# Split halves for a gated linear attention's gates, and the order of two feed-forward heads

## The chip, the cores and the metric

The kernel runs on one core of one Trainium2 chip. Its time is the device time of one execution in microseconds (us). The core has five engines, which the profile calls PE (TensorE, matrix products; its weight loads are listed as PEld), DVE (VectorE), ACT (ScalarE), POOL (GpSimd) and SP (SyncE, which here only issues DMA transfers). Each has its own queue of instructions and takes them in order; they wait for one another through semaphores.

## The reference

The reference is a trunk of four layers over 512 rows of 1024 numbers. A layer adds a mixer and then a feed-forward network (FFN) to `x`, each on a normalised copy. The mixers are S5 (layers 0 and 3), gated linear attention (GLA, layer 1) and differential attention (layer 2). All is in float32. What the change touches:

```python
def swiglu_ffn(h, w_gate_up, w_down):
    g, u = jnp.split(h @ w_gate_up, 2, axis=-1)
    return (jax.nn.silu(g) * u) @ w_down

# in gla_mixer: chunks of 64 rows, 4 heads with 128 keys and 256 values each
log_a = jax.nn.log_sigmoid((a_lo @ w_a2 + b_a).astype(f32)) / GLA_TEMP
cum = jnp.cumsum(log_a.reshape(shp_k), axis=2)
tot = cum[:, :, -1]
k_dec = k * jnp.exp(tot[:, :, None] - cum)
upd = jnp.einsum('bnchk,bnchv->bnhkv', k_dec, v)
decay = jnp.exp(tot)
# state = decay * state + upd, chunk after chunk; o = q @ state
```

`a_lo` has 16 columns; `w_a2` is 16 x 512 and `b_a` has 512 numbers. The FFN's hidden width is 2816.

## The kernel before

**Split halves.** A float32 operand is split into a high half (a cast to the type float32r, on ScalarE, line 420) and a low half (the rest, a subtraction on VectorE, line 428). A product is then three matmuls: high by high, high by low, low by high (`mm3`, lines 448 to 450; `seven_product`, line 594). Halves of weights lie in `whl`, which has five buffers. Weights come as raw tiles by DMA, some of them summed in the transfer (an accumulating DMA from POOL, lines 626 and 759).

**Seven products for eight.** The FFN's first matrix product and GLA's projection run in blocks of 256 columns by a scheme of Strassen's kind: seven quarter products, which the code calls one to seven, in place of eight. Each takes 24 matmuls of 256 columns. The left side's quarters and their sums (sides 11, 12, 22, and the totals 1 to 4) are made once; each block splits its own weights 11, 1, 21, 22 and 3, adds 22 to weight 1 and splits it again (S in the plans), adds 21 and splits it a third time (F). A suffix a, b or c names block 0, 1 or 2, and `one:a` is block a's product one, `one_out:a` its way out of the accumulator. In an FFN a block ends in `scale1` and `silu1` (first gate half), `gate2` (scale and silu of the second), `three_out` and `times` (gate by value, for each half) and `parts`, which splits the result into `act` for the down projection (`gemm_b`).

**The order of the work.** A planner orders every engine's instructions at compile time from a model of their costs, by the order in which the code emits them. Between `hand(...)` calls the engines that it names follow the emitted order exactly. `issue_after` ties an instruction behind another one on its engine. Each FFN begins with a plan written out by hand, the string `plan` in `ffn` (blocks a and b, engines PE, ACT, DVE, SP and POOL), and then a second one, which brings in block c and the gates of a and b (PE, ACT and DVE); from block c's `six` on the planner decides. FFNs 0 and 3 are called `glued`: they lay out their memory in another way.

**GLA.** Blocks 0 and 1 of the projection follow a plan of their own; from there on the order of TensorE alone is written out, and `block(b, out, between)` runs seven products with steps of the attention between them. Block 2 makes half the keys (`kd`), block 3 the values of two heads (`v1`). The gate steps: `alo` is `a_lo` turned, 32 rows because both halves of its weights are stacked; `decays` multiplies it by `w_a2` (line 2284, a plain float32 matmul over 128 rows, most of them zero or one) and takes Abs, Exp and Ln for the log-sigmoid; `sums` finishes that into `la`. `totals` forms each chunk's total with 16 matmuls that have `la` standing still and a two-column indicator `ind` streaming (line 2308), which gives them with the keys in partitions, as `dec` needs them; `later` forms the suffix sums with a triangular `mask` standing still and `la` streaming (line 2299) and multiplies the keys by their exponentials. `updates` and `readout` are the recurrence.

**FFN 2** also turns `x` and `r` through DRAM (`turn_x`, POOL), since S5 behind it wants its rows in another order. The side sum `total("3")` of that FFN is made at the end of the attention (line 2798).

Of the kernel before, what the change touches and what calls it, by code (L numbers as in the profile page):

```python
# [22 lines left out]
P = 128  # L23
D = 1024
# [316 lines left out]
class Trunk:  # L341
# [387 lines left out]
    def seven_block(self, fp, slots, left, wgu, b, turn, na):  # L729
# [35 lines left out]
        third = lambda name: self.np_.tile([P, 512], F32, tag="h", name=name) if b == 2 else T(name)  # L765
# [120 lines left out]
    def ffn(self, l, left, after=None, turn=False, aside=None, small=None):  # L886
# [7 lines left out]
        with self.tc.tile_pool(name=f"ffn{l}", bufs=1, reuse_waits="tile") as fp:  # L894
# [12 lines left out]
            blocks = [self.seven_block(fp, slots, left, wgu, b, turn, na) for b in range(FFN_HIDDEN // 256)]  # L907
# [10 lines left out]
            if l == 2:  # L918
                plan = """
                    split21a one:a split21b square flush one:b total1 one_out:a finish high1 low1 total2 split1a  # L920
# [3 lines left out]
                    high22 low22 three:a add21a highFa add21b lowFa highFb three:b lowFb seven_out:b scale1:a four:a  # L924
                    four:b
                """
            else:
# [6 lines left out]
                """  # L934
            def turned():
                nonlocal r
                r = self.turn_x(left.r) if turn else r
# [21 lines left out]
            self.planned(plan, left, f, more)  # L959
# [3 lines left out]
            for nb in (4, 4, 3) if na == 4 else (3, 3, 3, 2):  # L963
                acts = []
                for n in range(b0, b0 + nb):
                    b = blocks[n]
                    if n > 2:
                        loads(b)
                        for step in ("one", "one_out", "five", "five_out"):
                            b[step]()  # L970
                        b["add"]("22")
# [6 lines left out]
                    with self.tc.issue_after(behind["low"].ins) if n < 2 else nullcontext():  # L978
                        acts.append(b["parts"]())
# [1125 lines left out]
    def gla(self, l, left, after):  # L2105
# [5 lines left out]
        with self.tc.tile_pool(name="gla", bufs=1, reuse_waits="tile") as p:  # L2111
# [8 lines left out]
            on = [None, room("N", "on1")]  # L2120
# [33 lines left out]
            class Rows:  # L2154
# [17 lines left out]
                def stt(_, th, half, ps, f, op):  # L2172
                    for t, o, y in _.each(th, half, ps):
                        v.scalar_tensor_tensor(o, y, f[:, t : t + 1], o, op0=ALU.mult, op1=op)
# [32 lines left out]
            nc.gpsimd.dma_start(xd[:, :, 512:], self.x[:, :, 512:])  # L2207
# [36 lines left out]
            aT, wa2 = flat[:, :512], flat[:, 512:1024]  # L2244
# [7 lines left out]
            for n in (32, 64, 96):  # L2252
                v.memset(aT[n : n + 32], 1.0)
            nc.gpsimd.memset(wa2, 0.0)
            nc.sync.dma_start(wa2[0:16], i["gla_w_a2"][0])
            nc.sync.dma_start(wa2[16:32], i["gla_w_a2"][0])
            nc.sync.dma_start(wa2[32:33], i["gla_b_a"][0:1])
# [11 lines left out]
            v.tensor_tensor(aT[:32], ap_[:32], R[:32], op=ALU.mult)  # L2269
# [3 lines left out]
            on[0] = room("B", "on0")  # L2273
            la = room("D", "la")
# [3 lines left out]
            logs = []  # L2278

            def decays():  # L2280
                zs = [row(bank) for bank in four("z")]
                es = [flat[:, 1024 + t * 512 : 1536 + t * 512] for t in range(NT)]
                for t, (z, e) in enumerate(zip(zs, es)):
                    nc.tensor.matmul(z, aT[:, t * P : (t + 1) * P], wa2[:], start=True, stop=True)
# [7 lines left out]
            def sums():  # L2292
                with self.tc.issue_after(self.last["rows"].ins):
                    for t, (z, e) in enumerate(logs):
                        v.scalar_tensor_tensor(la[:, t], z, 0.0, e, op0=ALU.min, op1=ALU.subtract)

            def later():
                for t, bank in enumerate(four("suf")):
                    nc.tensor.matmul(row(bank), mask[:], la[:, t], start=True, stop=True)
# [4 lines left out]
            def totals():  # L2304
                dps = self.tp("dps")
                for t in range(NT):
                    for h in range(4):
                        nc.tensor.matmul(
                            dps[:, t, 2 * h : 2 * h + 2], la[:, t, h * P : (h + 1) * P], ind[:], start=True, stop=True
                        )  # L2310
                src = dps[:, :, :8].rearrange("p t (h c) -> p t h c", c=2)
                nc.scalar.activation(dec[:], src, AF.Exp, scale=1.0 / 16.0)
# [99 lines left out]
            block(2, Rows(kd, None, True), (decays, pause, sums, pause, pause, totals))  # L2412
            vs[1] = room("D", "v1")
            block(3, Rows(vs[1]), (later, pause, *core(0)))
# [83 lines left out]
    def diff(self, l, left, after):  # L2498
# [4 lines left out]
        with self.tc.tile_pool(name="diff", bufs=1) as p:  # L2503
# [289 lines left out]
            for t in range(2):  # L2793
# [4 lines left out]
                3: {1: (one,), 3: (one, lambda: nxt[0].total("3")), 5: (one,)},  # L2798
# [68 lines left out]
```

## Time and profile before

| | us |
|---|---|
| median of 3 runs (2232.98 to 2233.42) | 2233.0 |
| the profiled execution | 2241.29 |
| its span, first to last instruction | 2239.5 |
| TensorE busy | 2177.8 |
| VectorE busy | 1629.1 |
| ScalarE busy | 1139.5 |

The mean granted TensorE clock was 0.996 of full speed. Stages by TensorE's rows: S5 to about 207 us, FFN 0 to 567, GLA to 778, FFN 1 to 1120, differential attention to 1394, FFN 2 to 1737, S5 to 1895, FFN 3 to 2231.

How to read the rows: a timeline row has a start (us from the span's start), a length, the engine, the code line, the operation, what it writes and reads, the shape and a count; rows that follow one another are merged. The bracket at its end is the engine's idle time before it and who ended that. TensorE's matmuls overlap one another, so what one costs is read from start to start. A row of a chain gives start, length and what ran or was waited for.

### The profile page before, as it was taken

Reading aid. Unit: us, or ns where it says so; the run is one execution under the profiler, and the core shown is the slowest. Engines: PE = TensorE matmul, PEld = TensorE weight load, DVE = VectorE, ACT = ScalarE, POOL = GpSimd, SP = SyncE. Lnnn points to the kernel's source line nnn. Section 1 sums busy time; section 2 is a strip of 40 time slices with the busy share of each in tenths; the row PEclk is TensorE's granted clock in tenths of the full one; section 3 lists DMA queues with packets and bytes.
Section 4 is the critical chain, followed back from the end, with each engine's and each line's share of the span. In section 5 each row is a group of like instructions: output and inputs, shape, how many; then the busy total and the mean of one; then the engine's idle time right before and its main releaser. Section 6 shows DMA issues by size and latency. Waiting matters only on the chain.

```text
span 2239.5 us, 38455 instructions
## 1 busy us (share of the span) xinstructions
PE 2177.8 (97%) x15433; PEld 1973.2 (88%) x15433; DVE 1629.1 (73%) x2497; ACT 1139.5 (51%) x1835; POOL 330.0 (15%) x441
## 2 busy tenths in 40 slices
PE   6999999999999999999999999899999999999998
PEld 5888889989988898999888888899998888989997
DVE  9965978777978598876745676877766965967675
ACT  8644635445555455564435675644544334535343
POOL 3401142340111010100002221100000001101000
PEclk9999999999999999999999999999999999999999
DMA  4357667665763675765337455975631546856532
GB/s 92 63 172 179 180 156 195 161 172 169 175 141 113 155 183 171 178 186 129 94 129 166 108 134 150 248 194 132 179 95 57 155 147 160 199 159 166 164 76 76
DMA packets 309181, 333.63 MB, mean 149 GB/s; under 512 B 70477, under 2 KB 253033, under 8 KB 308874
## 3 DMA queue, kind: packets, MB, share of 16 engines
q1 hardware_dynamic: 238970, 238.93, 34.7%
q0 software_dynamic: 70032, 92.23, 21.9%
q8 instruction: 122, 2.00, 0.4%
q14 instruction: 57, 0.47, 0.1%
HBM read 297.16 MB, written 18.75 MB: 141 GB/s over the span
## 4 chain that ended last, share of the span: by engine, by line
PE 78%; DVE 10%; ACT 4%; issue 3%; DMA 3%; SPq 1%; POOL 0%; DVEq 0%; ACTq 0%; POOLq 0%
PE a L594 20%; PE acc L448 10%; PE acc L450 10%; PE acc L449 10%; PE c L594 10%; PE d L594 5%; DVE whl L428 3%; PE y L1651 2%; PE acc L1687 2%; ACT whl L420 2%; DMA halves<-in_ffn_w_gate_up_dram 1%; PE op L2650 1%; PE s L2617 1%; PE tp L117 1%; PE V L1607 1%
## 5 line engine op out<-in xcount | busy, mean ns | idle before, releaser
L428 DVE TENSOR_TENSOR whl<-wst,whl 128x1024 fp32r<-128x1024 f32 x260 | 316.6, 1223 | 213.4 <-ACT whl L420 209.9
L594 PE MATMUL a<-side,whl 128*128 128x256 f32 x3240 | 396.2, 279 | 10.2 <-DVE whl L428 7.4
L420 ACT CAST whl<-wst 128x1024 fp32r<-128x1024 f32 x260 | 272.2, 1051 | 241.7 <-PE acc L450 153.5
L594 PEld LDWEIGHTS a<-side,whl 128*128 128x128 f32 x3240 | 382.1, 189 | 13.9 <-DVE whl L428 9.5
L448 PE MATMUL acc<-whl,act 128*128 128x512 f32 x704 | 276.2, 392 | 0.4 <-DVE g L770 0.2
L449 PE MATMUL acc<-whl,act 128*128 128x512 f32 x704 | 274.6, 390 | 0.0
L450 PE MATMUL acc<-whl,act 128*128 128x512 f32 x704 | 274.4, 390 | 0.0
L594 PE MATMUL c<-side,whl 128*128 128x256 f32 x2160 | 261.3, 277 | 4.4 <-ACT whl L420 4.4
L594 PEld LDWEIGHTS c<-side,whl 128*128 128x128 f32 x2160 | 253.0, 188 | 5.0 <-ACT whl L420 5.0
L428 DVE TENSOR_TENSOR whl<-slot,whl 128x1024 fp32r<-128x1024 f32 x105 | 127.7, 1221 | 61.6 <-ACT whl L420 61.0
L448 PEld LDWEIGHTS acc<-whl,act 128*128 128x128 f32 x704 | 132.1, 188 | 29.3 <-DVE x L576 0.9
L450 PEld LDWEIGHTS acc<-whl,act 128*128 128x128 f32 x704 | 132.2, 188 | 27.6
L449 PEld LDWEIGHTS acc<-whl,act 128*128 128x128 f32 x704 | 132.2, 188 | 26.4
L420 ACT CAST whl<-slot 128x1024 fp32r<-128x1024 f32 x105 | 109.9, 1052 | 84.9 <-PE acc L450 44.6
L594 PE MATMUL a<-sides,whl 128*128 128x256 f32 x1080 | 132.9, 278 | 1.0 <-DVE x L576 1.0
L428 DVE TENSOR_TENSOR whl<-halves,whl 128x1024 fp32r<-128x1024 f32 x87 | 105.8, 1222 | 37.4 <-ACT whl L420 37.1
L420 ACT CAST whl<-halves 128x1024 fp32r<-128x1024 f32 x87 | 90.8, 1050 | 81.2 <-DVE halves L824 35.7
L594 PE MATMUL d<-sides,whl 128*128 128x256 f32 x1080 | 131.1, 278 | 0.0
L594 PEld LDWEIGHTS a<-sides,whl 128*128 128x128 f32 x1080 | 128.3, 188 | 2.2 <-issue 1.4
L594 PEld LDWEIGHTS d<-sides,whl 128*128 128x128 f32 x1080 | 127.5, 188 | 0.0
L759 POOL DMA_DIRECT2D wst<-in_ffn_w_gate_up_dram x44 | 57.1, 1297 | 463.8 <-DMA wst<-in_ffn_w_gate_up_dram 206.9
L877 ACT CAST act<-r 128x512 fp32r<-128x512 f32 (+1 forms) x110 | 66.7, 644 | 97.6 <-DVE r L853 80.5
(511 smaller groups left out, 4030.5 us busy)
## 6 DMA issues: line engine op xcount, KB each, us to landing
wst<-in_ffn_w_gate_up_dram SPq DMA_DIRECT2D x88, 512.0 KB, 4.9
wst<-in_ffn_w_down_dram SPq DMA_DIRECT2D x88, 512.0 KB, 4.5
slot<-in_ffn_w_gate_up_dram SPq DMA_DIRECT2D x69, 512.0 KB, 6.3
wst<-in_ffn_w_gate_up_dram POOLq DMA_DIRECT2D x44, 512.0 KB, 6.0
halves<-in_ffn_w_gate_up_dram SPq DMA_DIRECT2D x42, 512.0 KB, 6.1
wst<-in_s_w_glu_dram SPq DMA_DIRECT2D x32, 512.0 KB, 4.7
wst<-in_diff_w_qkv_dram SPq DMA_DIRECT2D x24, 512.0 KB, 4.9
slot<-in_ffn_w_gate_up_dram POOLq DMA_DIRECT2D x18, 512.0 KB, 8.9
```

The costliest lines, as they stand in the source:

```text
L117: tr.nc.tensor.transpose(p[:, j], h[:, j * P : (j + 1) * P], tr.ident[:])
L420: self.last["high"] = self.nc.scalar.copy(hl[:, 0], w[:])
L428: self.last["low"] = self.nc.vector.tensor_tensor(hl[:, 1], w[:], hl[:, 0].bitcast(F32), op=ALU.subtract)
L448: mm(out, lh, rh, start=first, stop=False)
L449: mm(out, lh, rl, start=False, stop=False)
L450: self.last["mm"] = mm(out, ll, rh, start=False, stop=last)
L594: mm(o, *two, start=first and not (j or k or n), stop=k == 3 and n == 2, skip_group_check=True,)
L759: nc.gpsimd.dma_start(w[:], left.quarter(*plus, b), accum_op=ALU.add)
L877: self.last["act high"] = nc.scalar.copy(dst[:, 0, j], src[:, j])
L1607: mm(V[kk][z][:, bs(b)], inm[:, z, bs(b)], U[:, bs(b)], start=True, stop=True)
L1651: mm(yb[:, b], q[:, j, b], om[:, j // 2, bs(b)], start=False, stop=j == 3)
L1687: mm(accs[t][:], zT[:, m // 2, kk, t * P : (t + 1) * P], hl[:, m % 2, kk % 2], start=kk == 0 and m == 0, stop=kk == KT - 1 and m == 2,)
```

## The change

In FFNs 1 and 2 the second written plan is dropped. In FFN 1 the first plan's end is reordered: scale and silu of both blocks come before the sum and splits for `four`, `three_out` of both after `four`; behind it come `gate2`, `times` and `parts` of a, then of b, then all of block c, in the planner's hands. In FFN 2 scale, silu and `three_out` are drawn into the first plan in the same way, behind the splits; then block c's loads and the split of its weight 1 come before gate a, its products one and five, the sum and the second split before gate b. Block c's results use the FFN's own buffers there. `total("3")` moves from the attention's end into FFN 2's plan. FFNs 0 and 3 keep both plans.

In GLA the gates, totals and suffix sums become products on split halves. `aT` stacks the high half, the low half and the high half of `a_lo`, and two rows of ones; `wa2` stacks high, high and low halves of the weights and both halves of the bias, so that one matmul over 98 rows per row tile gives the gates. The log gates are split into `lhi` and `llo` (`highs` on ScalarE, `lows` on VectorE, between blocks 2 and 3). The totals are formed with an eight-column window of the indicator standing still and 512 columns of `lhi` and `llo` streaming, eight matmuls that add up to an 8 x 512 tile, chunks in rows; its exponential is turned by four small transposes (`spread`). They move from block 2, behind its product three, to block 3, behind its product one, ahead of the suffix sums, which take two matmuls per tile in place of one.

```diff
@@ -726,7 +726,7 @@
-    def seven_block(self, fp, slots, left, wgu, b, turn, na):
+    def seven_block(self, fp, slots, left, wgu, b, turn, na, glued):
@@ -762,7 +762,7 @@
-        third = lambda name: self.np_.tile([P, 512], F32, tag="h", name=name) if b == 2 else T(name)
+        third = lambda name: self.np_.tile([P, 512], F32, tag="h", name=name) if glued and b == 2 else T(name)
@@ -904,7 +904,7 @@
-            blocks = [self.seven_block(fp, slots, left, wgu, b, turn, na) for b in range(FFN_HIDDEN // 256)]
+            blocks = [self.seven_block(fp, slots, left, wgu, b, turn, na, glued) for b in range(FFN_HIDDEN // 256)]
@@ -917,12 +917,12 @@
-                    split21a one:a split21b square flush one:b total1 one_out:a finish high1 low1 total2 split1a
+                    split21a one:a split21b square flush one:b total3 total1 one_out:a finish high1 low1 total2 split1a
...
-                    high22 low22 three:a add21a highFa add21b lowFa highFb three:b lowFb seven_out:b scale1:a four:a
-                    four:b
+                    high22 low22 three:a add21a highFa add21b lowFa highFb three:b lowFb seven_out:b scale1:a silu1:a four:a
+                    scale1:b silu1:b four:b three_out:a three_out:b
@@ -932,6 +932,13 @@
                 """
+            if l == 1:
+                a = plan.index("seven_out:b")
+                plan = plan[:a] + """
+                    seven_out:b scale1:a silu1:a scale1:b silu1:b add21a high22 low22 three:b highFa add21b lowFa highFb
+                    lowFb four:a four:b three_out:a three_out:b
+                """
+
             def turned():
@@ -956,7 +963,8 @@
-            self.planned(plan, left, f, more)
+            if glued:
+                self.planned(plan, left, f, more)
@@ -964,7 +972,18 @@
                     b = blocks[n]
-                    if n > 2:
+                    if not glued and n < 2:
+                        if l == 2 and n == 0:
+                            loads()
+                            blocks[2]["split"]("1")
+                        if l == 2 and n == 1:
+                            for step in ("one", "one_out", "five", "five_out"):
+                                blocks[2][step]()
+                            blocks[2]["add"]("22")
+                            blocks[2]["split"]("1")
+                        for step in ("gate2", "times"):
+                            b[step]()
+                    if n > 2 or l == 1 and n == 2:
                         loads(b)
@@ -975,7 +994,7 @@
                             b[step]()
-                    with self.tc.issue_after(behind["low"].ins) if n < 2 else nullcontext():
+                    with self.tc.issue_after(behind["low"].ins) if glued and n < 2 else nullcontext():
                         acts.append(b["parts"]())
@@ -2117,7 +2136,7 @@
-            on = [None, room("N", "on1")]
+            on = [None, None]
@@ -2171,7 +2190,9 @@
-                        v.scalar_tensor_tensor(o, y, f[:, t : t + 1], o, op0=ALU.mult, op1=op)
+                        self.last["added"] = v.scalar_tensor_tensor(
+                            o, y, f[:, t : t + 1], o, op0=ALU.mult, op1=op
+                        )
@@ -2204,7 +2225,7 @@
-            nc.gpsimd.dma_start(xd[:, :, 512:], self.x[:, :, 512:])
+            begun = nc.gpsimd.dma_start(xd[:, :, 512:], self.x[:, :, 512:])
@@ -2241,7 +2262,6 @@
-            aT, wa2 = flat[:, :512], flat[:, 512:1024]
@@ -2249,12 +2269,26 @@
-            for n in (32, 64, 96):
-                v.memset(aT[n : n + 32], 1.0)
-            nc.gpsimd.memset(wa2, 0.0)
-            nc.sync.dma_start(wa2[0:16], i["gla_w_a2"][0])
-            nc.sync.dma_start(wa2[16:32], i["gla_w_a2"][0])
-            nc.sync.dma_start(wa2[32:33], i["gla_b_a"][0:1])
+            exact = lambda y: y.bitcast(F32R)
+            zpart = whole(room("N", "zpart"))
+            aT, wa2, win, inner = (zpart[:, a:b] for a, b in ((0, 512), (512, 1024), (1024, 1038), (1040, 1168)))
+            wraw, araw = flat[:, 3072:3584], flat[:, 3584:4096]
+            wlow = self.sp.tile([P, 2], F32, tag="ms2", name="wlow", bufs=4)
+            nc.gpsimd.memset(araw[96:128], 1.0)
+            with self.tc.issue_after(begun.ins):
+                nc.gpsimd.memset(wlow[64:96, 0:1], -1.0)
+                nc.gpsimd.tensor_scalar_mul(wlow[96:128, 0:1], self.ident[96:128, 97:98], -1.0)
+            wa = i["gla_w_a2"][0]
+            nc.sync.dma_start(
+                wraw[0:96], bass.AP(tensor=wa.tensor, offset=wa.offset, ap=[[0, 6], [512, 16], [1, 512]])
+            )
+            nc.sync.dma_start(wraw[96:98], i["gla_b_a"][0].partition_broadcast(2))
+            nc.scalar.copy(exact(wa2[:98]), wraw[:98])
+            v.scalar_tensor_tensor(
+                wraw[64:98], wa2[64:98], wlow[64:98, 0:1], wraw[64:98], op0=ALU.mult, op1=ALU.add
+            )
+            nc.scalar.copy(exact(wa2[64:98]), wraw[64:98])
+            nc.scalar.copy(exact(aT[96:98]), araw[96:98])
@@ -2266,22 +2300,25 @@
-            v.tensor_tensor(aT[:32], ap_[:32], R[:32], op=ALU.mult)
+            v.tensor_tensor(araw[:32], ap_[:32], R[:32], op=ALU.mult)
+            for n in (0, 64):
+                nc.scalar.copy(exact(aT[n : n + 32]), araw[:32])
+            v.tensor_tensor(exact(aT[32:64]), araw[:32], aT[:32], op=ALU.subtract)
...
-            on[0] = room("B", "on0")
-            la = room("D", "la")
+            lhi, llo = room("D", "lhi"), room("B", "llo")
...
+            tot = flat[:8, 512:1024]
...
-                    nc.tensor.matmul(z, aT[:, t * P : (t + 1) * P], wa2[:], start=True, stop=True)
+                    nc.tensor.matmul(z, exact(aT[:98, t * P : (t + 1) * P]), exact(wa2[:98]), start=True, stop=True)
@@ -2292,24 +2329,44 @@
-                        v.scalar_tensor_tensor(la[:, t], z, 0.0, e, op0=ALU.min, op1=ALU.subtract)
+                        v.scalar_tensor_tensor(e, z, 0.0, e, op0=ALU.min, op1=ALU.subtract)
+                    v.tensor_copy(exact(inner), mask[:])
+                    v.tensor_scalar_mul(exact(win), mask[:, :14], 0.0)
+                    v.tensor_copy(exact(win[:, 6:8]), ind[:])
+
+            def highs():
+                for t in range(NT):
+                    nc.scalar.copy(exact(lhi[:, t]), logs[t][1])
+
+            def lows():
+                for t in range(NT):
+                    v.tensor_tensor(exact(llo[:, t]), logs[t][1], lhi[:, t], op=ALU.subtract)
...
+                totals()
...
-                    nc.tensor.matmul(row(bank), mask[:], la[:, t], start=True, stop=True)
+                    for z, y in enumerate((lhi, llo)):
+                        nc.tensor.matmul(row(bank), exact(inner), exact(y[:, t]), start=z == 0, stop=z == 1)
...
-                dps = self.tp("dps")
+                dps = row(self.tp("dps"))[:8]
...
-                    for h in range(4):
+                    for z, y in enumerate((lhi, llo)):
...
-                            dps[:, t, 2 * h : 2 * h + 2], la[:, t, h * P : (h + 1) * P], ind[:], start=True, stop=True
+                            dps, exact(win[:, 6 - 2 * t : 14 - 2 * t]), exact(y[:, t]),
+                            start=not (t or z), stop=t == NT - 1 and z == 1,
...
-                src = dps[:, :, :8].rearrange("p t (h c) -> p t h c", c=2)
-                nc.scalar.activation(dec[:], src, AF.Exp, scale=1.0 / 16.0)
+                nc.scalar.activation(tot, dps, AF.Exp, scale=1.0 / 16.0)
+
+            def spread():
+                dps = self.tp("dct")
+                for h in range(4):
+                    nc.tensor.transpose(dps[:, h, :8], tot[:, h * P : (h + 1) * P], self.ident[:8, :8])
+                v.tensor_copy(dec[:], dps[:, :, :8].rearrange("p h (t c) -> p t h c", c=2))
+                on[:] = room("B", "on0"), room("N", "on1")
@@ -2409,9 +2466,13 @@
-            block(2, Rows(kd, None, True), (decays, pause, sums, pause, pause, totals))
+            block(2, Rows(kd, None, True), (decays, pause, sums))
+            with self.tc.issue_after(self.last["high"].ins):
+                highs()
+            with self.tc.issue_after(self.last.pop("added").ins):
+                lows()
...
-            block(3, Rows(vs[1]), (later, pause, *core(0)))
+            block(3, Rows(vs[1]), (later, spread, *core(0)))
@@ -2795,7 +2856,7 @@
-                3: {1: (one,), 3: (one, lambda: nxt[0].total("3")), 5: (one,)},
+                3: {1: (one,), 3: (one,), 5: (one,)},
```

## The prediction

> **What bounds the kernel now.** I read first the page's busy times and its chain that ended last, then the busy time by stretch of the three places that the change touches (GLA, 567 to 778 us; the heads of FFN 1, up to 850, and of FFN 2, 1394 to 1470), then the engines' timelines there.
>
> ```profile
> PE 2177.8 (97%) x15433; PEld 1973.2 (88%) x15433; DVE 1629.1 (73%) x2497; ACT 1139.5 (51%) x1835; POOL 330.0 (15%) x441
> PE 78%; DVE 10%; ACT 4%; issue 3%; DMA 3%; SPq 1%; POOL 0%; DVEq 0%; ACTq 0%; POOLq 0%
> ```
>
> TensorE is the bound: busy 97% of the span, 78% of the chain. A change pays if it shortens TensorE's list or removes one of its few waits, and costs if it puts VectorE (10% of the chain) or ScalarE ahead of it. The profiled execution took 2241.29 us, of which the span is 2239.5; the median of the runs is 2233.0, so it ran 8.3 us longer. I form the differences on the profiled execution and apply them to the median.
>
> **GLA: what the products cost.** The timeline of TensorE, a row per product (start, length, and in brackets, where there is one, the idle time before it and who ended it):
>
> ```profile
> 615.87 3.59 PE L2284 MATMUL z<-work 128*128 128x512 f32 x8
> 618.90 3.39 PE L594 MATMUL c<-whl,side 128*128 128x256 f32 x24
> ...
> 630.62 2.99 PE L594 MATMUL c<-whl,side 128*128 128x256 f32 x24
> 633.45 4.22 PE L2308 MATMUL dps<-ind,la 128*128 128x2 f32 x32
> 637.54 5.47 PE L594 MATMUL a<-whl,side 128*128 128x256 f32 x24
> 642.80 3.07 PE L594 MATMUL a<-whl,sides 128*128 128x256 f32 x24
> 645.71 3.59 PE L2299 MATMUL suf<-la,mask 128*128 128x512 f32 x8
> 648.74 3.39 PE L594 MATMUL c<-whl,side 128*128 128x256 f32 x24
> ```
>
> From start to start: the four gate products (`z`, two records each) take 3.03 us, the 16 totals (`dps`) 4.09, the four suffix sums (`suf`) 3.03. A quarter product of 24 matmuls takes 2.83 (630.62 to 633.45), but the one behind the totals 5.26. A split-half product of 512 columns is priced by the output projection of the attention:
>
> ```profile
> 1365.84 0.40 PE L448 MATMUL acc<-whl,oT 128*128 128x512 f32 x1
> ...
> 1367.67 0.39 PE L450 MATMUL acc<-whl,oT 128*128 128x512 f32 x1
> ```
>
> Eight steps in 1.83 us, 0.229 each. So: gates 4 x 0.229 = 0.92, saving 2.1. Totals 8 x 0.229 = 1.83, and `spread` four small transposes, between 0 and 0.5 (a matmul of 256 columns is 2.83 / 24 = 0.118), I take 0.4: 2.2, saving 1.9. Suffix sums 8 x 0.229 = 1.83, saving 1.2. Together 5.2 us of TensorE, all on the path.
>
> The Trainium skill (FP8 and Floating Point Precision, TensorE Precision Notes) counts four passes for true FP32. By that a gate product or a suffix sum would cost 4 x 0.229 = 0.92 now and the two savings would come to 2.75 and 1.8; the trace has 0.76 a product (3.03 / 4), and I go by the trace.
>
> **GLA: the clock.** Busy time by stretch (PE, PEld, DVE, ACT, POOL, then granted clock, DMA share and GB/s):
>
> ```profile
> 613.00:620.00 7.00, 7.00 (x41) 5.08 (x40) 6.50 (x9) 6.57 (x8) 1.28 (x1) 1.00 0.55 111
> 620.00:626.00 6.00, 6.00 (x53) 6.00 (x52) 2.76 (x6) 5.97 (x11) 0.00 (x0) 1.00 0.93 284
> 626.00:633.00 7.00, 7.00 (x62) 7.00 (x61) 7.00 (x12) 4.37 (x5) 1.28 (x1) 1.00 0.62 111
> 633.00:640.00 7.00, 7.00 (x49) 7.00 (x48) 2.40 (x4) 2.07 (x3) 1.28 (x1) 0.74 0.46 128
> 640.00:646.00 6.00, 6.00 (x40) 5.90 (x39) 2.96 (x4) 1.10 (x2) 0.00 (x0) 0.74 0.47 74
> ```
>
> With the two-column totals the granted clock falls to 0.74 on average until 646; that is the 5.26 against 2.83. The new totals stream 512 columns like the products around them, so I take the drop to go: another 2.4 us (bounds: 0, if eight active columns count as idle too, and 3.4, 0.26 x 13, with the part inside `dps`).
>
> **GLA: what is added beside it.** ScalarE: five copies for `aT` and `wa2`, four casts for `lhi`. VectorE: four subtractions for `llo`, one for `aT`, one step for `wa2`, small copies, less three memsets. Two of these end in a wait of TensorE, whose order is written out here.
>
> ```profile
> 613.33 0.68 DVE L2269 TENSOR_TENSOR work<-alo,R 32x512 f32<-32x512 f32 x1
> 613.40 1.05 ACT L420 CAST whl<-gain 128x1024 fp32r<-128x1024 f32 x1 [2.16 <-DVE gain L674]
> 634.44 1.22 DVE L674 TENSOR_TENSOR halves<-halves 128x1024 f32<-128x1024 f32 x1
> 643.04 0.88 DVE L2168 TENSOR_SCALAR kd<-a,rcol 128x256 f32<-128x256 f32 x2 [7.38 <-PE a L594]
> ```
>
> (a) `z` now waits for VectorE's multiply (done at 614.0), a copy on ScalarE (free at 614.5; some 0.6 for half the columns of the 1.05) and a subtraction on VectorE (0.68), the last perhaps behind a low half of 1.2: near 616.7, not 615.87, +0.8 (bounds 0 and 2.5, with both copies and a cast ahead). (b) `lows` is tied behind the last step of `three_out`, and stands on VectorE ahead of block 3's first low half, for which TensorE's `one` waits; behind `one` come totals and suffix sums. `three` now ends 1.3 us earlier (2.1 - 0.8), at 632.2; `three_out` (0.9 for two) to 633.4, four subtractions of 0.65 to 636.0, the low half to 637.2, against `one` due at 632.2 + 2.83 = 635.0: +2.2. Its bounds are 0, if the planner puts that low half first, and 3.1 with `four_out` (0.88) ahead too. After that VectorE has cover: it stands idle for 7.38 us now. ScalarE is full from 613 to 626 and two copies more delay `sums` by 1.2 us; nothing for TensorE, whose next need of them comes 15 us later. SP has two small loads in place of three, POOL three tiny steps behind its store of x; its next accumulation comes 20 us later. GLA: -5.2 - 2.4 + 0.8 + 2.2 = -4.6.
>
> **FFN 1's head.** Only order changes: both gates' scale and silu go ahead of the last splits, `three_out` behind `four`, then everything from the second gates on is left to the planner, which takes over one block earlier. Block c's five loads and two accumulations keep their place on SP and POOL, since gates and parts issue no transfer. Two stretches, then VectorE's and TensorE's timeline:
>
> ```profile
> 801.00:812.00 11.00, 11.00 (x99) 11.00 (x98) 10.71 (x11) 6.57 (x8) 1.28 (x1) 1.00 0.78 221
> 831.00:838.00 7.00, 5.67 (x31) 5.06 (x30) 6.35 (x8) 2.65 (x5) 1.28 (x1) 0.76 0.95 156
> 811.40 1.23 DVE L428 TENSOR_TENSOR whl<-lent,whl 128x1024 fp32r<-128x1024 f32 x1
> 813.37 5.66 PE L594 MATMUL a<-side,whl 128*128 128x256 f32 x48
> 825.59 2.78 PE L594 MATMUL a<-side,whl 128*128 128x256 f32 x22 [0.76 <-DVE whl L428]
> 832.56 0.50 PE L594 MATMUL c<-side,whl 128*128 128x256 f32 x2 [0.32 <-ACT whl L420]
> 833.93 4.39 PE L594 MATMUL a<-side,whl 128*128 128x256 f32 x22 [0.87 <-DVE whl L428]
> ```
>
> VectorE is full. The low half of block a's `four` is done at 812.6; the new order puts two scales (1.3), one more sum (1.2) and the wait for the silus (0.6, estimated from the copy above) ahead of it: 815.7, and `four` (813.37, its third matmul) waits 2 us. The gates are then further on when block c begins, so the waits at 825 to 834 (1.95 us in three rows) shrink by as much. VectorE's total is the same: 0 for the waits (bounds -2, and +5.2 if the two gates' eight steps of 0.65 come ahead of the splits and nothing is won back). The clock of 0.76 over 7 us lost 1.7; the new wait can lose it again, I take half: -0.8.
>
> The Trainium skill (TensorE: Matmul & The Clock Gate, Why this matters for your kernels) asks that TensorE have no idle gap of more than some 3 us. By that none of the new waits would cost clock and the term would be -1.7; here the clock fell after waits of under 1 us each, so I don't rely on it.
>
> **FFN 2's head.** The order to `lowFb` stays but for `total3`. Behind it scale, silu and `three_out` of both blocks come early; block c's split of weight 1 is ahead of gate a, its second split ahead of gate b, the rest planned; loads keep their place. VectorE, TensorE, and two pieces of the chain:
>
> ```profile
> 1431.90 1.22 DVE L428 TENSOR_TENSOR whl<-wst,whl 128x1024 fp32r<-128x1024 f32 x1
> 1437.71 1.23 DVE L824 TENSOR_TENSOR halves<-halves 128x1024 f32<-128x1024 f32 x1 [1.46 <-DMA halves<-in_ffn_w_gate_up_dram]
> 1435.27 2.88 PE L594 MATMUL a<-sides,whl 128*128 128x256 f32 x24
> 1442.13 0.50 PE L594 MATMUL a<-side,whl 128*128 128x256 f32 x2 [1.26 <-ACT whl L420]
> 1443.39 2.77 PE L594 MATMUL a<-side,whl 128*128 128x256 f32 x22 [0.76 <-DVE whl L428]
> 1450.49 0.50 PE L594 MATMUL a<-side,whl 128*128 128x256 f32 x2 [1.11 <-ACT r L835]
> 1454.78 0.80 PE L594 MATMUL c<-side,whl 128*128 128x256 f32 x2 [3.78 <-ACT whl L420]
> 1443.71 9.86 DMA halves<-in_ffn_w_gate_up_dram
> 1455.57 4.15 PE a L594 x22
> ```
>
> Four waits, 1.26 + 0.76 + 1.11 + 3.78 = 6.9 us, and the product after them at half clock, 4.15 for 22 matmuls, not 2.6: 1.55 more. The longest is no lack of work: two matmuls of the next block's `five` (x2) stand in TensorE's order ahead of 22 of block c's own, and their weights land at 1453.6. That landing doesn't move. If VectorE has worked off the gates by then, the planner's order is plain, and c's seven, three, four and the next `one` (4 x 2.83 = 11.3 us) cover it: -3.78 - 1.55 - 1.11. At `six`, two waits of 2.0 go, since the gates no longer stand behind a sum that waits for its load. In exchange block c's first low half (1433.1 now, used at 1435.3: 2.2 early) stands behind a scale, two `three_out`, a low half and a gate (0.65 + 2.4 + 1.2 + 0.65 = 4.9): +2.7 at `one` (bound 0: the planner finds a gap), some of it cover for `six`, so I take 2.3, and 0.7 at `six` for what is left. FFN 2: -6.4 - 2.0 + 3.0 = -5.4 (bounds -8.5 and +3).
>
> `total3`, two VectorE steps, moves from the attention's tail into this plan:
>
> ```profile
> 1393.98 1.29 DVE L223 TENSOR_TENSOR s<-halves 128x512 f32<-128x512 f32 x2
> 1404.65 1.22 DVE L428 TENSOR_TENSOR whl<-lent,whl 128x1024 fp32r<-128x1024 f32 x1
> 1405.92 1.30 PE L594 MATMUL c<-side,whl 128*128 128x256 f32 x10
> ```
>
> VectorE is free 1.2 us earlier at 1394, of which the sum behind it can use some 0.5, as it waits for its own product; so the low half ending at 1405.87 comes 0.7 later, and `five` at 1405.92 had it just in time: +0.6 (bounds 0 and 1.3).
>
> Sum: -4.6 - 0.8 - 5.4 + 0.6 = -10.2: 2231.1 for the profiled execution, 2222.8 for the median.
>
> **The rivals.** *The late `five` stays.* The planner still puts heads of the next block ahead while VectorE is behind, and TensorE waits for 1453.6 whatever it saved before. For it: in FFN 1 too the first products after the planner takes over (832.56) are such heads. FFN 2 gives back 3.78 + 1.55: -4.9, 2228.1. *Gates first starve the splits (slower).* VectorE is full, 5.2 us of gates stand ahead of block c's splits and are not won back in either FFN, each with a half clock like the 1.7 at 831; 2 x 6.9 - 4.6 + 0.6 = +9.8, 2243. It decides from about 2.5 us of lasting wait per FFN. Against it: those gates stood ahead of block c's third product already. *It doesn't do what it says.* The casts and waits eat the GLA gain (`z` 2.5, lows 3.1, a half clock of 3.4 from them: +9.0 on -7.6) and the FFNs trade wait for wait: +1 to +2, 2235.
>
> **How the numbers follow.** Forecast 0.44, late `five` 0.22, nothing won 0.13, slower 0.21. A measurement of this kernel tells changes above about 0.2%, 4.5 us, from none. The late-`five` case lies at that edge: 0.19 of it goes to faster, 0.03 to same; of nothing won 0.1 to same, 0.01 to faster, 0.02 to slower: faster 0.64, same 0.13, slower 0.23. The time is 2223; its own range is 2214 (GLA at -7.6 + 0.6, FFN 2 at -8.5) to 2228. Over the cases, leaving out the worse half of the slower one, 2213 to 2240.
>
> **What would show it.** Clock 1.00 behind the totals; from `z` to the next product about 0.9, totals and suffix sums 3.7 together; `one` of block 3 waiting about 2 us for VectorE; no x2 heads with a 4 us wait near 1450. It is wrong if block c's `one` in either FFN waits over 3 us for L428, or a half-clock stretch follows `z`.

## The result, and the profile after

The changed kernel takes 2229.58 us (median of 19 runs, 2227.02 to 2234.96), the kernel before, run beside it, 2234.26 (19 runs, 2231.90 to 2238.52): a ratio of 0.9978 with a 95% interval of 0.9971 to 0.9984. That is 4.7 us (3.6 to 6.5) less, where 10.2 less was forecast. The time lies above the forecast's own range (2214 to 2228) and inside the one over all its cases (2213 to 2240). The sign is right, and the size is 46% of the forecast one.

The page of the changed kernel: busy times, then the chain that ended last by engine.

```profile
PE 2166.7 (97%) x15409; PEld 1964.6 (88%) x15409; DVE 1631.7 (73%) x2504; ACT 1145.4 (51%) x1844; POOL 332.2 (15%) x443
PE 79%; DVE 10%; ACT 5%; issue 3%; DMA 1%; POOL 1%; SPq 0%; DVEq 0%; POOLq 0%; ACTq 0%
```

DMA's share of the chain falls from 3% to 1%; TensorE's is as it was (78% before). This execution took 2228.83 us, 0.75 under its median. The profiled execution of before took 2241.29, and ran 7 us over the median of the kernel's 19 runs. So the two profiled executions differ by 12.5 us, the medians by 4.7.

The timeline of TensorE in GLA, after:

```profile
613.14 2.90 PE L594 MATMUL a<-whl,sides 128*128 128x256 f32 x24
617.24 1.17 PE L2321 MATMUL z<-zpart 98*128 98x512 f32 x4 [1.21 <-ACT whl L420]
618.25 2.99 PE L594 MATMUL c<-whl,side 128*128 128x256 f32 x24
...
638.04 0.40 PE L2358 MATMUL dps<-lhi,zpart 128*8 128x512 f32 x1
...
639.90 0.40 PE L2349 MATMUL suf<-lhi,zpart 128*128 128x512 f32 x1
...
642.59 0.50 PE L2349 MATMUL suf<-lhi,zpart 128*128 128x512 f32 x1 [1.15 <-ACT work L2362]
642.93 0.39 PE L2349 MATMUL suf<-llo,zpart 128*128 128x512 f32 x1
643.16 2.89 PE L594 MATMUL c<-whl,side 128*128 128x256 f32 x24
645.99 0.41 PE L2367 MATMUL dct<-ident,work 8*128 8x8 f32 x4
646.32 3.01 PE L594 MATMUL a<-whl,side 128*128 128x256 f32 x24
```

The gates take 1.01 from start to start (3.03 before), the totals 1.86 and the four transposes 0.33, the suffix sums 3.26 with a wait of 1.15 in them. The busy time by stretch (PE, PEld, DVE, ACT, POOL, then granted clock, DMA share, GB/s) has the clock at 1.00 behind the totals; here before stood 0.74.

```profile
636.00:643.00 7.00, 5.85 (x35) 4.13 (x34) 4.92 (x7) 4.32 (x6) 1.28 (x1) 1.00 0.51 75
643.00:650.00 7.00, 7.00 (x60) 6.63 (x60) 6.89 (x9) 6.35 (x13) 0.65 (x1) 1.00 0.33 92
```

TensorE at FFN 1's head and at FFN 2's, after:

```profile
809.96 5.50 PE L594 MATMUL a<-side,whl 128*128 128x256 f32 x46 [1.73 <-DVE whl L428]
...
819.51 2.78 PE L594 MATMUL c<-side,whl 128*128 128x256 f32 x22 [1.10 <-DVE whl L428]
...
823.28 0.50 PE L594 MATMUL d<-sides,whl 128*128 128x256 f32 x2 [0.44 <-ACT whl L420]
```

```profile
1399.46 5.68 PE L594 MATMUL c<-side,whl 128*128 128x256 f32 x46 [0.51 <-DVE whl L428]
...
1433.47 2.86 PE L594 MATMUL a<-sides,whl 128*128 128x256 f32 x22 [1.15 <-DVE whl L428]
...
1437.77 0.50 PE L594 MATMUL d<-sides,whl 128*128 128x256 f32 x2 [1.21 <-ACT whl L420]
```

FFN 1 has its 1.73 at `four:a` and two more waits behind it. FFN 2 has no late `five` and no half clock; what is left at block c are two small waits, at `one` (1.15) and at `two` (1.21).

### The profile page after: what moved, and what is told of

It is laid out like the page before. It is cut to its first block, busy times and chain, and to the rows that moved or that the text cites. A ratio compares the mean times of both kernels' runs of the same rounds, so it can differ in the third digit from the quotient of the medians.

```text
span 2227.1 us, 38431 instructions
## 1 busy us (share of the span) xinstructions
PE 2166.7 (97%) x15409; PEld 1964.6 (88%) x15409; DVE 1631.7 (73%) x2504; ACT 1145.4 (51%) x1844; POOL 332.2 (15%) x443
## 4 chain that ended last, share of the span: by engine, by line
PE 79%; DVE 10%; ACT 5%; issue 3%; DMA 1%; POOL 1%; SPq 0%; DVEq 0%; POOLq 0%; ACTq 0%
PE a L594 20%; PE acc L448 11%; PE acc L450 11%; PE acc L449 11%; PE c L594 10%; PE d L594 6%; DVE whl L428 2%; PE y L1670 2%; ACT whl L420 2%; PE acc L1706 2%; PE op L2711 1%; PE s L2678 1%; PE tp L117 1%; PE V L1626 1%; PE acc L2766 1%
```

## How the runs were read

Beside the timed ratio, each trace gives three lengths, from the start of one matmul to the start of another that is the same in all: GLA (from the first of the last eight transposes of FFN 0 to the first `op` of the readout), FFN 1's head (from the first of the last eight transposes of GLA to the first matmul of the down projection) and FFN 2's head (the same behind the differential attention). `total3` counts in the last.

| kernel | median us (before beside it) | ratio, 95% | GLA | FFN 1 | FFN 2 | rest |
|---|---|---|---|---|---|---|
| before, first profile | | | 91.27 | 83.78 | 90.89 | 1973.5 |
| e1 before again | 2234.98 (2236.44) | 0.9993 (0.9985 to 1.0002) | 89.66 | 81.80 | 88.65 | 1972.0 |
| e2 GLA alone | 2231.81 (2236.44) | 0.9979 (0.9970 to 0.9988) | 85.55 | 81.65 | 91.75 | 1974.6 |
| e3 FFN 1 alone | 2235.97 (2236.44) | 0.9998 (0.9990 to 1.0007) | 89.65 | 83.58 | 88.51 | 1971.4 |
| e4 FFN 2 alone | 2232.45 (2236.44) | 0.9978 (0.9969 to 0.9987) | 89.61 | 81.81 | 85.85 | 1972.0 |
| after | 2229.58 (2234.26) | 0.9978 (0.9971 to 0.9984) | 85.45 | 82.78 | 86.16 | 1972.7 |
| e5 after again | 2230.08 (2235.11) | 0.9983 (0.9974 to 0.9992) | 85.53 | 82.80 | 86.74 | 1972.4 |
| e6 GLA and FFN 2 | 2228.88 (2235.11) | 0.9970 (0.9959 to 0.9981) | 85.46 | 81.66 | 86.10 | 1971.8 |
| e7 other order in FFN 1 | 2229.83 (2235.11) | 0.9978 (0.9969 to 0.9987) | 85.46 | 84.75 | 85.90 | 1971.3 |
| e8 early table | 2227.40 (2235.11) | 0.9970 (0.9959 to 0.9982) | 84.12 | 81.65 | 85.90 | 1975.5 |
| e9 totals in rows, fp32 | 2235.11 (2235.64) | 0.9995 (0.9987 to 1.0004) | 88.78 | 83.26 | 89.10 | 1971.4 |
| e10 two-column totals | 2233.21 (2235.64) | 0.9986 (0.9977 to 0.9996) | 88.28 | 81.80 | 86.73 | 1975.9 |
| e11 best | 2227.27 (2235.64) | 0.9959 (0.9946 to 0.9973) | 84.15 | 81.66 | 85.05 | 1973.1 |
| e12 FFN 1, splits first | 2227.96 (2235.64) | 0.9963 (0.9951 to 0.9976) | 85.47 | 81.67 | 85.84 | 1973.1 |
| e13 both in FFN 1 | 2227.66 (2236.02) | 0.9962 (0.9948 to 0.9976) | 84.15 | 82.16 | 85.43 | 1974.7 |

The rest differs by up to 4.6 us between executions, of kernels whose code there is the same, for the most part through half-clock stretches at other places. That, and the 1.5 us between two loads of one program (e1), is the grain of a single comparison. The three lengths are finer: in GLA the same code agrees within 0.1 us (89.61 to 89.66 in e1, e3 and e4), a second piece of half clock aside.

## The experiments

**e1: the kernel before, a second time.** No edit.

> The kernel before, unchanged, profiled a second time. Theory A (the first profiled execution of it, 2241.29 us at a mean clock of 0.996, was not a typical one): mean clock 0.998 or higher in nearly every run, a profiled time of 2232 to 2236, and in the new trace the 3.78 us wait of block c's next five near 1450 us and the 4.15 us product behind it are gone, or much shorter, and one or two of the three half-clock stretches (636, 834, 1452 us) are missing. Theory B (these waits stand in every execution of before, and the changed kernel loses its gain elsewhere): clock 0.996, the wait of 3 to 4 us near 1450 there again, and all three stretches.

Half of each. FFN 1's half clock (834 us) is gone, and the totals' is 3.41 us long, not 6.83. But the mean clock is 0.996, and the late `five` is there, 2 us long, with the half clock behind it. TensorE's timeline, and the chain that led to it:

```profile
1446.25 0.79 PE L594 MATMUL c<-side,whl 128*128 128x256 f32 x2 [1.95 <-ACT whl L420]
1446.84 4.89 PE L594 MATMUL a<-side,whl 128*128 128x256 f32 x22
```

```profile
1417.79 16.30 DMA halves<-in_ffn_w_gate_up_dram
...
1434.38 10.67 DMA halves<-in_ffn_w_gate_up_dram
...
1446.25 0.79 PE c L594 x2
```

So the stall belongs to the kernel, and its size to the execution: it is the landing of an accumulating DMA. Five executions with the old order of FFN 2 waited 2.0, 2.1, 3.4, 3.8 and 4.0 us for it; FFN 2's head took 88.5 to 91.8. The accumulation itself takes 9.9 to 11.0 us in the five. The plain load into the same tile, behind which it is issued, takes 16.3 (e1) to 18.8 (e2), so more of the spread lies in that load.

**e2, e3, e4: the parts alone.** e2 takes the changed `gla` alone. e3 and e4 take one FFN's order each, with a flag in place of `glued`:

```
+ old = l in (0, 3) or l == 2        # e3: FFN 1 new;  e4: l in (0, 3) or l == 1, with total3 moved
- if glued: self.planned(plan, left, f, more)
+ if old: self.planned(plan, left, f, more)
```

> GLA's part alone; both FFN heads and the place of total3 as before. The pair of traces shows -5.4 us over GLA (5.6 by the first readout). Theory A: the products' own saving of 4 to 5 us less the two new waits (1.4 at z, 1.3 at the last suffix sum) is -2.5 to -3, and as much of the 2.4 us of half clock behind the totals as a usual execution has: -3 to -5.4, so nearly the whole measured change of -4.7. Theory B: -5.4, with the rest of the change (-0.3 -6) lost again.

> FFN 1's order alone. The pair of traces shows -1.0. Theory A: the 1.9 us wait at block a's four is new, the waits behind it shrink by as much, and the half clock of 1.7 us at 834 is not in every execution: between -1 and +1. Theory B: -1.0.

> FFN 2's order alone, with total3 in its plan. The pair of traces shows -6 and +0.7. Theory A: the late five (3.78) and its half clock (1.55) are not in a usual execution of before, so this is -1 to +1. Theory B: -5, that is 2229. If the order itself is slow (the rival with gates ahead of the splits): +2 or more.

GLA is worth 4.1 to 4.2 in each trace (85.5 against 89.65). FFN 1 costs: 82.8 to 83.6 against 81.7 without a half clock; the time of e3 alone (0.9990 to 1.0007) is too coarse to show it. FFN 2 with `total3` is worth about 3: 85.8 to 86.7 in new order, 88.5 to 91.8 in old. Neither theory of e1 holds whole. In time the parts come to -4.6, -0.5 and -4.0 against the kernel before beside them, -9 in all, and to -3.2, +1.0 and -2.5, -4.7 in all, against e1; the second sum is that of the whole. Which is right the ratios alone don't settle; the lengths give -4.2 + 1.1 - 3.1 = -6.2 (medians of all traces, FFN 1 without its half clocks). FFN 1 before, from e1:

```profile
822.99 2.86 PE L594 MATMUL a<-side,whl 128*128 128x256 f32 x22 [0.60 <-DVE whl L428]
...
829.95 0.50 PE L594 MATMUL c<-side,whl 128*128 128x256 f32 x2 [0.32 <-ACT whl L420]
831.33 2.78 PE L594 MATMUL a<-side,whl 128*128 128x256 f32 x22 [0.87 <-DVE whl L428]
```

1.79 us of idle time before, 1.73 + 1.10 + 0.44 = 3.27 after: the new waits don't replace the old ones one for one.

**e5, e6: after again, and without FFN 1's part.** e6 is the changed kernel with FFN 1 in its old order (`old = l in (0, 3) or l == 1`).

> The changed kernel again, unchanged, so that the next three can be held against it on the same chip. Theory P (the whole is the sum of its parts: GLA -4, FFN 2 -2.5 to -4, FFN 1 +1): 4 to 6 us under the kernel before. Theory Q (the parts get in each other's way, -4.7 and -4.9 alone but only -4.7 together, while FFN 1 is neutral): the same -4.7, so this run alone doesn't tell the two apart. In the trace: FFN 1's waits of 1.9, 1.3 and 0.6 us (808, 818, 823) again, and no wait above 1.5 us behind 1440.

> GLA's and FFN 2's parts together, FFN 1 as in the kernel before. Theory P: 1.0 to 1.3 us faster than the changed kernel, since FFN 1's three new waits come to 3.8 us and the old ones, which come back, to 2.3 to 2.8 us. Theory Q: the same as the changed kernel within 0.5, or slower. By the prediction's term for FFN 1 (-0.8) it would be 0.8 slower.

e6 is 1.2 us faster than the changed kernel beside it, which is within the grain, but its FFN 1 is 81.66, not 82.80: theory P. In the lengths the parts add up: GLA is 85.55 alone (e2) and 85.45 in the whole, FFN 2 85.85 alone (e4) and 86.16 in the whole, and FFN 1 costs 1.1 in the whole too.

**e7, e12, e13: FFN 1's order.** e7 puts the last low halves ahead of the scales; e12 brings block c's splits ahead of the gates, as in FFN 2; e13 does both, on e11's kernel.

```
  # e7 and e13, FFN 1's first plan behind seven_out:b
- scale1:a silu1:a scale1:b silu1:b add21a high22 low22 three:b highFa add21b lowFa highFb lowFb four:a four:b ...
+ high22 add21a low22 highFa lowFa scale1:a silu1:a three:b add21b highFb lowFb four:a scale1:b silu1:b four:b ...
  # e12 and e13, the loop over blocks
- if l == 2 and n == 0:                # and: if l == 2 and n == 1:
+ if n == 0:                           # and: if n == 1:
- if n > 2 or l == 1 and n == 2:
+ if n > 2:
```

> The changed kernel with one thing different: in FFN 1's first order block a's last low half stands ahead of the two scales again (block b's too), and the gates still go ahead of block c's splits. If the 1.9 us wait at block a's four comes from the two scales and the sum ahead of that low half, it goes; the waits behind it (1.3 and 0.6) may grow by what VectorE still has to do, so the trace should show between -1.9 (nothing comes back) and 0 (all of it). If the wait comes from something else (the silus on ScalarE, a load), it stays at 1.9.

> The changed kernel with FFN 1's second part made as FFN 2's is: block c's loads and its split of weight 1 ahead of gate a, its product five and the second split ahead of gate b. Block a's four still waits 1.9 us. Theory (FFN 1 loses because gates and parts, some 8 steps of 0.65 us, stand ahead of block c's splits on a VectorE that is full): the waits of 1.3 and 0.6 near 818 and 823 shrink to 0.5 or less together, and FFN 1 is 1 to 1.5 faster than in the changed kernel, level with the kernel before. Rival (VectorE's backlog is paid wherever the steps stand, as the other order with its 0.5 and 3.3 suggests): as much wait turns up some products later, and the sum over FFN 1's head stays within 0.5 of 3.8.

> All that helped so far (GLA's and FFN 2's parts, the early Exp table, total3 in the attention's tail), and FFN 1 with both of its parts changed: block a's and b's last low halves ahead of the scales, and block c's splits ahead of the gates. Theory (FFN 1's loss is order alone, two scales and a sum ahead of four's low half, gates and parts ahead of block c's splits): the 1.9 at four falls to 0.5 and nothing above 0.7 stands behind it, FFN 1's head is 1 to 1.5 shorter than in the kernel before, and the whole comes to 2225.5 to 2226.5. Rival (VectorE is full and the wait at four only moves, as with the one order changed, where 0.5 and 3.3 took the place of 1.9, 1.3 and 0.6): 2 us or more of wait at block c's five or two, and no gain over FFN 1 as before.

TensorE's waits at FFN 1's head, e7, then e12, then e13:

```profile
810.20 2.78 PE L594 MATMUL a<-side,whl 128*128 128x256 f32 x22 [0.37 <-DVE whl L428]
...
819.08 4.39 PE L594 MATMUL c<-side,whl 128*128 128x256 f32 x22 [3.15 <-DVE whl L428]
```

```profile
809.06 5.50 PE L594 MATMUL a<-side,whl 128*128 128x256 f32 x46 [1.74 <-DVE whl L428]
...
820.66 0.50 PE L594 MATMUL d<-sides,whl 128*128 128x256 f32 x2 [0.39 <-ACT whl L420]
```

```profile
809.50 2.78 PE L594 MATMUL a<-side,whl 128*128 128x256 f32 x22 [0.36 <-DVE whl L428]
...
813.04 3.00 PE L594 MATMUL c<-side,whl 128*128 128x256 f32 x24 [0.53 <-DVE r L852]
816.58 2.79 PE L594 MATMUL a<-sides,whl 128*128 128x256 f32 x22 [0.53 <-DVE whl L428]
820.40 3.12 PE L594 MATMUL a<-side,whl 128*128 128x256 f32 x24 [1.03 <-ACT r L800]
```

e7: the wait at `four:a` is the two scales and the sum, as the prediction had it; taken away there, it comes back at block c's `five`, with a half clock (4.39 for 22 matmuls). e12: with c's splits ahead of the gates the later waits shrink from 1.54 to 0.39, and FFN 1 is level with before (81.67). e13: 0.36 + 0.53 + 0.53 + 1.03 = 2.45 and 82.16, worse than e12 alone, and not the 1 to 1.5 under the old order that was expected. So gates ahead of splits are what the changed order loses by, and the rival is right too in its way: with VectorE full, no order tried came under the old one's 81.7.

**e8, e11: an Exp table ahead of time, and `total3` back.** In the changed kernel the last suffix sum waits for line 2362, the Exp of the totals, whose bank it takes over. ScalarE there, after:

```profile
638.65 2.00 ACT L420 CAST whl<-halves 128x1024 fp32r<-128x1024 f32 x2 [6.63 <-DVE halves L674]
640.66 1.28 ACT L2362 ACT_TABLE_LOAD   x1
641.95 0.59 ACT L2362 ACTIVATE work<-dps 8x512 f32<-8x512 f32 x1
```

e8 is e6 with one more instruction, e11 is e8 with `total("3")` back in the attention's tail.

```
+ early = self.sp.tile([P, 2], F32, tag="ms2", name="early", bufs=4)
+ nc.scalar.activation(early[:], llo[:, 2, :2], AF.Exp)
```

> GLA's and FFN 2's parts together, and one more instruction: an Exp of two columns on ScalarE, whose result nobody uses, in the 6.6 us in which ScalarE is idle ahead of the totals, so that the table of Exp is loaded there. Theory: the last suffix sum's wait of 1.32 us is that load (1.28 us at 640.7, between the totals and the Exp that frees their bank); then the wait falls to 0.1 or less and the span by 1.2 to 1.3 against the same kernel without it. Rival: the wait is for the totals' own Exp and ScalarE's two casts ahead of it; then it shrinks by less than 0.5.

> GLA's and FFN 2's parts and the early load of the Exp table, with total3 back in the attention's tail as in the kernel before; FFN 1 as before. Against the same kernel with total3 in FFN 2's plan: the 0.68 us wait near 1397 goes (theory: two steps of VectorE ahead of that low half, as in the prediction), and nothing comes in its place, so 0.6 faster. Rival: the two steps cost TensorE something in the attention's tail, and it is level. Either way 2226.5 to 2228, about 3 us under the changed kernel.

In e8 the load lies in ScalarE's idle time and the Exp follows the casts directly:

```profile
631.56 1.28 ACT L2469 ACT_TABLE_LOAD   x1
...
640.10 0.58 ACT L2356 ACTIVATE work<-dps 8x512 f32<-8x512 f32 x1
```

The wait is gone and GLA is 84.12, not 85.46: the whole 1.3. In e11 TensorE starts FFN 2's first `five` without a break (after: 0.51 at 1399.46), and the head is 85.05 against 85.90.

```profile
1395.79 5.60 PE L594 MATMUL c<-side,whl 128*128 128x256 f32 x48
```

In time e8 is 1.5 us under e6 by the medians; their ratios, both 0.9970, are too coarse for it. At 2227.27, ratio 0.9959, e11 beats the kernel before by 0.27% at least, and the changed one by 2.3 to 2.8 us by the medians, 3.5 by the three lengths.

**e9, e10: what lets the clock fall.** e9 is the kernel before with rows of totals in fp32; e10 is e6 with the old totals.

```
  # e9                                                              # e10: the reverse, on logs[t][1]
- nc.tensor.matmul(dps[:, t, 2 * h : 2 * h + 2], la[:, t, h * P : (h + 1) * P], ind[:], start=True, stop=True)
+ nc.tensor.matmul(dps, win[:, 6 - 2 * t : 14 - 2 * t], la[:, t], start=t == 0, stop=t == NT - 1)
```

> The kernel before with one thing different: GLA's totals are four fp32 products of 512 columns that accumulate in rows, with the four small transposes behind, in place of 16 fp32 products of two columns; gates and suffix sums stay fp32, nothing is split. Theory (the two columns are what lets the clock fall): no half-clock stretch near 636, the product behind the totals at 2.8 us; the totals fall from 4.1 to about 3.0 (four products of 0.76), the transposes add 0.3, and with the 1.7 us of a half-clock stretch the GLA stretch gets 2 to 2.7 shorter. Rival (fp32 itself, or a wait near there, lets the clock fall): the stretch at 636 stays, and the gain is 0.8 at most.

> GLA's and FFN 2's parts together, but the totals as 16 fp32 products of two columns as in the kernel before (gates and suffix sums on split halves). Theory (two columns): the half clock behind the totals is back, 3.4 us or more of it, and the GLA stretch is longer by 1.7 for the clock and by 1.9 to 2.2 for the totals, less up to 1.3 if the last suffix sum's wait goes: 2.3 to 4 in all against the same kernel with totals in rows. Rival: the clock stays at 1.00, and only the products' own 2 us come back, less that wait.

The totals and the products behind them in e1's timeline and in e9's, then stretches of e9 and of e10:

```profile
632.28 3.63 PE L2308 MATMUL dps<-ind,la 128*128 128x2 f32 x32
635.77 4.60 PE L594 MATMUL a<-whl,side 128*128 128x256 f32 x24
640.21 2.88 PE L594 MATMUL a<-whl,sides 128*128 128x256 f32 x24
```

```profile
632.98 3.60 PE L2310 MATMUL dps<-la,work 128*8 128x512 f32 x8
636.51 3.01 PE L594 MATMUL a<-whl,side 128*128 128x256 f32 x24
639.36 2.88 PE L594 MATMUL a<-whl,sides 128*128 128x256 f32 x24
```

```profile
633.00:640.00 7.00, 7.00 (x39) 4.11 (x39) 5.74 (x7) 4.26 (x5) 1.28 (x1) 1.00 0.45 102
```

```profile
636.00:643.00 7.00, 7.00 (x45) 6.76 (x44) 2.88 (x3) 2.67 (x4) 1.29 (x1) 0.72 0.54 77
```

It is the two-column totals, not fp32: a half-clock stretch of 3.41 or 6.83 us starts in or just behind them in all five traces that have them, and in none of the ten that have rows. Nor is it their place, since e9's fp32 rows stand where the old totals stood, and e10's two columns where the new ones stand. What in the two-column products does it, the few streamed columns or a weight load for each of the sixteen, no run separates. e10's GLA is 2.8 us longer than e6's. e9 gained only 0.9, not 2 to 2.7: the product behind its totals takes 2.85 (4.44 in e1), but the 16 old totals take 3.49 in e1, not the 4.09 that I read in the first profile, so the rows (3.53) save nothing of their own, and the transposes cost 0.3; another 0.3 is spread over the other products.

## Why the prediction was right or wrong

**The step that failed first** is "I form the differences on the profiled execution and apply them to the median". Against that execution the terms come out well: GLA -5.8 (forecast -4.6), FFN 1 -1.0 (-0.8), FFN 2 with `total3` -4.7 (-4.8). But that execution had lost 1.6 us in GLA, 2.0 in FFN 1 and 2.2 in FFN 2 that e1 had not. The prediction saw that it "ran 8.3 us longer" and carried over every term whole, also the stalls that made it longer. Against e1 and the other traces:

**FFN 1: forecast -0.8, measured +1.1.** The -0.8 was half of a clock loss that seven of nine traces with the old order don't have. And "the waits at 825 to 834 shrink by as much" is false: the 2 us at `four:a` came as forecast, but 1.5 us of waits stand behind it, where 1.8 stood. The rival "gates first starve the splits" had the mechanism, though not its size: here in one FFN, at 1.1 us net (e12 takes just that back).

**FFN 2 with `total3`: forecast -4.8, measured -3.1** (86.0 against 89.1, medians). The mechanism was right: the late `five` and its half clock are in all five old traces and in none of the ten new ones, and the transfer comes no earlier (its accumulation starts 49.2 us into the stretch, 47.3 in e1). Block c's `one` and `two` wait in its place (1.15 and 1.21; forecast were 2.3 at `one` and 0.7 at `six`), `total3` costs 0.5 to 0.9 (forecast 0.6). The size was off: 3.78 was a late landing, 1.95 an early one. Against e1 TensorE's waits of over 0.1 us in that head fall by only 0.9, from 4.88 to 3.96 us, where the head gains 2.5: much of the gain is the half clock, 6.83 us long in e1, and not the waits. The rival "the late `five` stays" forecast 4.9 us less in all, close to the measured 4.7, but by chance: what it tells did not happen.

**GLA: forecast -4.6, measured -4.2**, with errors that cancel. Against e1: gates -2.0 (-2.1), suffix sums -1.1 without their wait (-1.2), totals with transposes -1.3 (-1.9, since 4.09 had half clock in it), clock -1.6 (-2.4). The products behind the old gates and suffix sums were 0.4 longer each (3.39 for 2.99), which went too: -0.8, not foreseen. Added are 1.3 at `z` (+0.8; it starts at 617.24, where 613.14 + 2.83 gives 615.97) and 1.3 at the last suffix sum (not foreseen: a table load). The forecast +2.2 at block 3's `one` is 0, its lower bound: the planner put both low halves of that block ahead of `lows`. VectorE, after:

```profile
631.09 1.23 DVE L428 TENSOR_TENSOR whl<-wst,whl 128x1024 fp32r<-128x1024 f32 x1
632.23 1.22 DVE L428 TENSOR_TENSOR whl<-halves,whl 128x1024 fp32r<-128x1024 f32 x1
633.37 0.87 DVE L2193 SCALAR_TENSOR_TENSOR kd<-c,rcol,kd 128x256 f32<-128x256 f32 x2
634.15 1.88 DVE L2343 TENSOR_TENSOR llo<-work,lhi 128x512 fp32r<-128x512 f32 x3
```

Together -4.2 + 1.1 - 3.1 = -6.2 in place of -10.2; 1.9 of the 4 us between them is FFN 1, 1.7 FFN 2. The medians show -4.7 and, the second time, -5.0; -6.2 lies within the first interval (6.5) and just outside the second (5.8). Whether the last 1.4 us are chance or a cost outside the three lengths stays open.

Of the signs named to watch, the clock behind the totals, the 0.9 of `z` (1.01) and the missing `five` came. The 2 us at block 3's `one` did not, and totals and suffix sums together took 5.12, not 3.7, for the table load; in e8, without it, they take 3.71. No wait of block c for line 428 reached the 3 us that would have spoken for the slower case. One sum of the prediction does not come out: the two terms named for 2214 give 2216.7 with FFN 1 at -0.8, and it takes FFN 1's lower bounds as well to get there.

## What to carry to other kernels

Before a stall or a half clock of one trace is counted as a gain, ask if it is in the code or in that execution: where the profiled run is slower than the median, the difference may sit in just such rows. Here 5.8 of the 7.3 us between the two profiles of the kernel before sat in the three heads, and the second would have shown GLA's half clock and the late `five` shorter and FFN 1's half clock gone. Where the engine that feeds the bound is full, taking work off one wait moves it to the next product, and what is needed first goes first: splits ahead of gates. Look at the table loads of ScalarE when its work is reordered; one of them stood between two matmuls here and cost 1.3 us.

## What the runs showed of the hardware

Wherever the half clock shows in the fifteen traces, it comes in a piece of 3.41 us, or two of them, the last few microseconds of the span aside; in three traces it shows nowhere else. Sixteen matmuls of two columns, each with its own weights, bring it on although TensorE's records fill the stretch (7.00 of 7.00 us busy in e10 at a clock of 0.72), and four of 512 columns don't. The Trainium skill (TensorE: Matmul & The Clock Gate, Part 1: The HAM clock gate) gives a window of 3413 ns that runs freely; the lengths here agree. Its table of the two states names an idle window as what brings the clock down, and the two-column stretch shows that busy records are no safeguard.

A table load on ScalarE took 1.28 us and the Exp behind it started at once (640.66 to 641.95). The Trainium skill (ScalarE: Activation LUTs, What ACT_TABLE_LOAD costs) counts about 1.38 more for a drain at each switch, 2.66 in all; here neither the rows nor the gain of e8, 1.3, show it.
